# A batched 64x64 matmul: both loads as fp32 from SyncE, casts moved to the engines, a two-stage pipeline

## The chip, the cores and the metric

One core of one Trainium2 chip. The metric is device time in microseconds (us) of that core. Most executions of a kernel agree within a fraction of a per cent; a run more than 1.5% above the fastest of its kernel is marked slow and is not used in a comparison. Rates are decimal GB/s; sizes of loads in KB and MB are powers of two, as the traces count them.

Some terms. HBM is the memory of the chip; SBUF is the core's own, in 128 partitions; PSUM is where TensorE (PE in the profile) leaves its results. A DMA is one copy between HBM and SBUF. An engine (GpSimd, SyncE or ScalarE) issues it, and the core's 16 DMA engines carry it out in packets. A load "lands" as its bytes reach SBUF. VectorE is DVE in the profile, ScalarE is ACT, GpSimd is POOL.

## The reference

```python
def setup_inputs():
    return {"a": np.random.randn(1024, 64, 64).astype(np.float32),
            "b": np.random.randn(1024, 64, 64).astype(np.float32)}

def reference(a, b):
    return np.matmul(a, b).astype(np.float32)
```

a, b and the output are 16.78 MB each, so 50.3 MB pass between HBM and the core, at very little arithmetic.

## The kernel before

The 1024 products are done in 16 tiles of 64. A tile of a is 1 MB, loaded in four DMAs (`h`) of 256 KB by GpSimd, which casts fp32 to bf16 on the way; a tile of b is one DMA of 1 MB by SyncE, still fp32, cast later by VectorE. Both sit in a pool of four tiles.

```python
    a_v = a.rearrange("(t g h) (mp v) k -> t h g mp (v k)", h=4, g=16, v=8)
    b_v = b.rearrange("(t g h) (kp u) n -> t (h kp) g (u n)", h=4, g=16, u=2)
    ...
    def load(t):
        a_sb = a_pool.tile([128, 4, 8, 64], bf16, name="a_sb")
        for h in range(4):
            nc.gpsimd.dma_start(
                out=a_sb[:, h, :, :].rearrange("p v k -> p (v k)"), in_=a_v[t, h]
            )
        b_sb = b_pool.tile([128, 16, 128], fp32, name="b_sb")
        nc.sync.dma_start(out=b_sb[:], in_=b_v[t])
    ...
    for t in range(n_t):
        load(t + AHEAD)                                   # if there is such a tile
        nc.vector.tensor_copy(a_bf[:], ...a_sb...)        # bf16 reorder
        # 16 transposes of a on PE, PSUM copied out half by VectorE, half by ScalarE
        for h in range(4):                                # block-diagonal weights
            nc.vector.tensor_copy(at_bd[rows, :, h, :], at_v[rows, :, :])
        nc.vector.tensor_copy(b_bf[:], b_sb[:])           # fp32 -> bf16
        for gq in range(4):
            ...                                           # 16 matmuls
            nc.scalar.copy(o_sb[:, gq, :, :, :], o_ps[:])
        nc.gpsimd.dma_start(out=o_v[t], in_=...o_sb...)   # 1 MB
```

(Cut and abridged: the comments with "..." stand for code that the argument does not touch.)

Of the kernel before, what the change touches and what calls it, by code (L numbers as in the profile page):

```python
# [1 line left out]

# [5 lines left out]

fp32 = mybir.dt.float32
bf16 = mybir.dt.bfloat16  # L10


@with_exitstack
def kernel(
    ctx: ExitStack,
    tc: tile.TileContext,
    a: bass.AP,
    b: bass.AP,
    out: bass.AP,
):  # L20





    nc = tc.nc
    B, M, K = a.shape
    _, _, N = b.shape
    assert (M, K, N) == (64, 64, 64) and B % 64 == 0

    T = 64
    n_t = B // T
    AHEAD = 3

    a_v = a.rearrange("(t g h) (mp v) k -> t h g mp (v k)", h=4, g=16, v=8)
    b_v = b.rearrange("(t g h) (kp u) n -> t (h kp) g (u n)", h=4, g=16, u=2)
    o_v = out.rearrange("(t g h) (mo w) n -> t (h mo) g (w n)", h=4, g=16, w=2)

    consts = ctx.enter_context(tc.tile_pool(name="consts", bufs=1))
    a_pool = ctx.enter_context(tc.tile_pool(name="a_pool", bufs=AHEAD + 1))  # L40
    b_pool = ctx.enter_context(tc.tile_pool(name="b_pool", bufs=AHEAD + 1))
    work = ctx.enter_context(tc.tile_pool(name="work", bufs=2))
    o_pool = ctx.enter_context(tc.tile_pool(name="o_pool", bufs=3))
    t_psum = ctx.enter_context(
        tc.tile_pool(name="t_psum", bufs=4, space=bass.MemoryType.PSUM)
    )
    o_psum = ctx.enter_context(
        tc.tile_pool(name="o_psum", bufs=4, space=bass.MemoryType.PSUM)
    )

    bd_tiles = [
        consts.tile([128, 64, 4, 32], bf16, name=f"at_bd{i}") for i in range(2)
    ]
    a_tiles, b_tiles = {}, {}

    def load(t):
        a_sb = a_pool.tile([128, 4, 8, 64], bf16, name="a_sb")
        for h in range(4):
            nc.gpsimd.dma_start(  # L59
                out=a_sb[:, h, :, :].rearrange("p v k -> p (v k)"), in_=a_v[t, h]  # L60
            )
        b_sb = b_pool.tile([128, 16, 128], fp32, name="b_sb")
        nc.sync.dma_start(out=b_sb[:], in_=b_v[t])
        a_tiles[t], b_tiles[t] = a_sb, b_sb

    load(0)
    identity = consts.tile([128, 128], bf16)
    make_identity(nc, identity)
    for bd in bd_tiles:
        nc.vector.memset(bd[:], 0.0)  # L70
    for t in range(1, AHEAD):
        load(t)

    for t in range(n_t):
        if t + AHEAD < n_t:
            load(t + AHEAD)
        a_sb, b_sb, at_bd = a_tiles.pop(t), b_tiles.pop(t), bd_tiles[t % 2]

        a_bf = work.tile([128, 8, 4, 64], bf16, name="a_bf")
        nc.vector.tensor_copy(a_bf[:], a_sb[:].rearrange("p h v k -> p v h k"))  # L80
        a_cols = a_bf[:].rearrange("p v h k -> p v (h k)")

        at_sb = work.tile([128, 2, 2, 128, 4], bf16, name="at_sb")
        for w in range(2):
            at_ps = t_psum.tile([128, 4, 2, 128], bf16, name="at_ps")
            for vo in range(4):
                for u in range(2):
                    nc.tensor.transpose(  # L88
                        at_ps[:, vo, u, :], a_cols[:, 2 * vo + w, u::2], identity[:]
                    )  # L90
            for u in range(2):
                dst = at_sb[:, w, u, :, :]
                src = at_ps[:, :, u, :].rearrange("p vo q -> p q vo")
                if u == 0:
                    nc.vector.tensor_copy(dst, src)  # L95
                else:
                    nc.scalar.copy(dst, src)  # L97
        at_v = at_sb[:].rearrange("p w u (g mp) vo -> p (w u g) (mp vo)", g=16)
        for h in range(4):
            rows = slice(32 * h, 32 * h + 32)  # L100
            nc.vector.tensor_copy(at_bd[rows, :, h, :], at_v[rows, :, :])  # L101
        b_bf = work.tile([128, 16, 128], bf16, name="b_bf")
        nc.vector.tensor_copy(b_bf[:], b_sb[:])  # L103
        o_sb = o_pool.tile([128, 4, 4, 2, 64], fp32, name="o_sb")
        for gq in range(4):
            o_ps = o_psum.tile([128, 4, 2, 64], fp32, name="o_ps")
            for g4 in range(4):
                g = 4 * gq + g4
                for w in range(2):
                    for u in range(2):  # L110
                        nc.tensor.matmul(  # L111
                            o_ps[:, g4, w, :],
                            at_bd[:, (2 * w + u) * 16 + g, :, :].rearrange(
                                "p h mo -> p (h mo)"
                            ),
                            b_bf[:, g, 64 * u : 64 * u + 64],
                            start=(u == 0),
                            stop=(u == 1),
                        )
            nc.scalar.copy(o_sb[:, gq, :, :, :], o_ps[:])  # L120

        nc.gpsimd.dma_start(  # L122
            out=o_v[t], in_=o_sb[:].rearrange("p q g w n -> p (q g w n)")
        )


# [1 line left out]
_INS = ['a', 'b']  # L128
_OUTS = [((1024, 64, 64), 'float32')]


# [23 lines left out]
```

## Time and profile before

| | before |
|---|---|
| time, median of 3 runs | 151.15 us |
| span of the profiled run | 148.9 us |
| busiest engines | VectorE 70% of the span, PE 43%, GpSimd 42%, ScalarE 36% |
| last load lands / last store lands | 121.6 / 147.1 us |

Parts of the profile page of the kernel before: busy times (us, share of the span, instructions), the busy tenths of the DMA engines in 40 slices, the GB/s of those slices, and the DMA queues (packets, MB, share of 16 engines' span).

```profile
PE 64.4 (43%) x1280; PEld 62.0 (42%) x1280; DVE 104.9 (70%) x130; ACT 53.5 (36%) x97; POOL 62.6 (42%) x86
...
DMA  3999999999999999999999999999999995892594
GB/s 77 292 290 292 291 293 293 295 286 276 293 364 383 322 291 275 370 308 290 283 348 366 309 292 287 368 310 291 294 321 369 195 356 207 237 273 68 169 265 129
...
q0 software_dynamic: 13568, 25.17, 66.7%
q1 hardware_dynamic: 8448, 16.78, 33.2%
```

The DMA row is full until about 123 us, and no engine is. So DMA bounds this kernel, then a tail does. The GB/s row needs care: it counts bytes **as they land**. Queue 0 carries 25.17 MB although it reads a (16.78 MB) and writes the output (16.78 MB): a counts at 8.39 MB, because it lands as bf16. So a slice with 292 GB/s and no stores reads more than 292 from HBM: counted in the trace's packet records from 8 to 32 us, 91 GB/s of a and 200 of b land, so 383 are read.

Two stretches of the same trace: without stores, and the tail. The columns are start:end, length, busy time of each engine, granted clock of PE, busy share of the DMA engines (over 1 when packets overlap), GB/s.

```profile
8.00:32.00 24.00, 11.84 (x192) 11.31 (x192) 16.95 (x22) 6.94 (x12) 10.09 (x17) 1.00 1.13 292
121.00:148.00 27.00, 13.91 (x285) 13.62 (x282) 13.78 (x20) 11.28 (x20) 4.92 (x4) 0.69 0.70 211
```

Two of the groups of instructions that the change touches (engine, operation, out<-in, shapes and types, count, then busy us, mean ns, then the engine's idle time just before them and what ended it):

```profile
L103 DVE CAST b_bf<-b_sb 128x2048 bf16<-128x2048 f32 x16 | 19.3, 1226 | 2.2 <-PE o_ps L111 2.2
L80 DVE COPY a_bf<-a_sb 128x2048 bf16<-128x2048 bf16 x16 | 10.8, 694 | 8.7 <-DMA a_sb<-in_a_dram 7.7
```

### The profile page before, as it was taken

The page shows a single profiled execution, that of the slowest core. Times are in us where ns is not written, and L with a number is a line of the kernel's source. Part 1 is how long each engine was busy: PE and PEld are TensorE (multiplying, and loading weights), DVE is VectorE, ACT ScalarE, POOL GpSimd, SP SyncE. Part 2 cuts the span into 40 slices and gives each one's busy share as a digit, 9 for nine tenths or more (in the row PEclk, how much of TensorE's full clock was granted, in tenths as well). Part 3 has the DMA queues.
Part 4 walks back from the last instruction along what each step waited for, and adds up shares of the span by engine and source line. Part 5 has one row for each costly group of instructions (what it writes and reads, how often), then busy time and mean ns, then how long its engine had stood idle before and what let it go on. Part 6 is the DMA issues. An engine that isn't in the chain of part 4 may idle for free.

```text
span 148.9 us, 3081 instructions
## 1 busy us (share of the span) xinstructions
PE 64.4 (43%) x1280; PEld 62.0 (42%) x1280; DVE 104.9 (70%) x130; ACT 53.5 (36%) x97; POOL 62.6 (42%) x86
## 2 busy tenths in 40 slices
PE   0005225960893058500990079402990059429400
PEld 0004215950893058500890078302880059429400
DVE  5754499799978297938995498919985497994000
ACT  3000052763320914064502733082602827616500
POOL 7644364336622165712983174614754303300410
PEclk9999999998569758955598557965599556975865
DMA  3999999999999999999999999999999995892594
GB/s 77 292 290 292 291 293 293 295 286 276 293 364 383 322 291 275 370 308 290 283 348 366 309 292 287 368 310 291 294 321 369 195 356 207 237 273 68 169 265 129
DMA packets 22031, 42.15 MB, mean 283 GB/s; under 512 B 1537, under 2 KB 9729, under 8 KB 22017
## 3 DMA queue, kind: packets, MB, share of 16 engines
q0 software_dynamic: 13568, 25.17, 66.7%
q1 hardware_dynamic: 8448, 16.78, 33.2%
q8 instruction: 10, 0.16, 0.4%
q14 instruction: 5, 0.03, 0.1%
HBM read 33.55 MB, written 16.78 MB: 338 GB/s over the span
## 4 chain that ended last, share of the span: by engine, by line
DMA 52%; issue 19%; POOL 11%; DVE 5%; PE 4%; ACT 3%; POOLq 1%; ACTq 0%; DVEq 0%
DMA a_sb<-in_a_dram 44%; POOL out_dram L122 8%; DMA out_dram<-o_sb 8%; PE o_ps L111 4%; POOL a_sb L59 2%; DVE at_sb L95 2%; DVE at_bd L101 2%; ACT at_sb L97 2%; ACT o_sb L120 1%; POOLq L150 1%; DVE b_bf L103 1%; DVE a_bf L80 0%; POOL identity masks.py:199 0%; POOL identity masks.py:197 0%; POOLq L122 0%
## 5 line engine op out<-in xcount | busy, mean ns | idle before, releaser
L111 PE MATMUL o_ps<-b_bf,at_bd 128*128 128x64 bf16 x1024 | 48.1, 225 | 59.3 <-DVE at_bd L101 59.3
L111 PEld LDWEIGHTS <-at_bd 128*128 128x128 bf16 x1024 | 46.6, 120 | 61.3 <-DVE at_bd L101 61.3
L59 POOL DMA_DIRECT2D a_sb<-in_a_dram x64 | 41.4, 652 | 50.8 <-DMA a_sb<-in_a_dram 23.7
L101 DVE COPY at_bd<-at_sb 32x2048 bf16<-32x2048 bf16 x64 | 49.7, 776 | 17.5 <-ACT at_sb L97 16.6
L120 ACT COPY o_sb<-o_ps 128x512 f32<-128x512 f32 x64 | 35.6, 591 | 65.7 <-PE o_ps L111 33.5
L122 POOL DMA_DIRECT2D out_dram<-o_sb x16 | 20.6, 1290 | 28.2 <-ACT o_sb L120 21.9
L97 ACT COPY at_sb<-at_ps 128x512 bf16<-128x512 bf16 x32 | 17.4, 624 | 20.2 <-DVE at_sb L95 20.0
L88 PE MATMUL at_ps<-identity,a_bf 128*128 128x128 bf16 x256 | 17.4, 231 | 15.8 <-DVE a_bf L80 15.8
L88 PEld LDWEIGHTS <-a_bf 128*128 128x128 bf16 x256 | 15.9, 104 | 16.1 <-DVE a_bf L80 16.1
L103 DVE CAST b_bf<-b_sb 128x2048 bf16<-128x2048 f32 x16 | 19.3, 1226 | 2.2 <-PE o_ps L111 2.2
L95 DVE COPY at_sb<-at_ps 128x512 bf16<-128x512 bf16 x32 | 19.9, 680 | 0.0
L80 DVE COPY a_bf<-a_sb 128x2048 bf16<-128x2048 bf16 x16 | 10.8, 694 | 8.7 <-DMA a_sb<-in_a_dram 7.7
L70 DVE MEMSET at_bd<- 128x4096 uint32 x2 | 6.9, 3472 | 2.5 <-PEq L139 1.7
L97 ACT ACT_TABLE_LOAD x1 | 1.3, 1283 | 0.7 <-PEq L139 0.7
masks.py:199 POOL TENSOR_SCALAR_AFFINE_SELECT identity<-identity 128x128 bf16<-128x128 bf16 x1 | 0.4, 364 | 0.0
masks.py:197 POOL MEMSET identity<- 128x128 bf16 x1 | 0.3, 266 | 0.0
L139 POOL MEMSET const-float32-0.0<- 128x1 f32 x1 | 0.1, 98 | 0.2 <-issue 0.2
L139 POOL MEMSET const-bfloat16-1.0<- 128x1 bf16 x1 | 0.1, 101 | 0.0
L139 POOL MEMSET const-uint8-127<- 128x1 uint8 x1 | 0.1, 101 | 0.0
L139 POOL MEMSET const-float32-1.0<- 128x1 f32 x1 | 0.1, 98 | 0.0
## 6 DMA issues: line engine op xcount, KB each, us to landing
out_dram<-o_sb POOLq DMA_DIRECT2D x16, 1024.0 KB, 10.9
a_sb<-in_a_dram POOLq DMA_DIRECT2D x64, 128.0 KB, 11.7
b_sb<-in_b_dram SPq DMA_DIRECT2D x16, 0.5 KB, 14.8
```

Source lines behind the costliest of these rows:

```text
L59: nc.gpsimd.dma_start(out=a_sb[:, h, :, :].rearrange("p v k -> p (v k)"), in_=a_v[t, h])
L70: nc.vector.memset(bd[:], 0.0)
L80: nc.vector.tensor_copy(a_bf[:], a_sb[:].rearrange("p h v k -> p v h k"))
L88: nc.tensor.transpose(at_ps[:, vo, u, :], a_cols[:, 2 * vo + w, u::2], identity[:])
L95: nc.vector.tensor_copy(dst, src)
L97: nc.scalar.copy(dst, src)
L101: nc.vector.tensor_copy(at_bd[rows, :, h, :], at_v[rows, :, :])
L103: nc.vector.tensor_copy(b_bf[:], b_sb[:])
L111: nc.tensor.matmul(o_ps[:, g4, w, :], at_bd[:, (2 * w + u) * 16 + g, :, :].rearrange("p h mo -> p (h mo)"), b_bf[:, g, 64 * u : 64 * u + 6 ...
L120: nc.scalar.copy(o_sb[:, gq, :, :, :], o_ps[:])
L122: nc.gpsimd.dma_start(out=o_v[t], in_=o_sb[:].rearrange("p q g w n -> p (q g w n)"))
L150: with _tile.TileContext(nc) as tc:
```

## The change

The intent: take the loads off GpSimd, so that it only issues stores; let SyncE issue both loads as plain fp32; split the casts between VectorE (a) and ScalarE (b); prepare tile t+1 before multiplying tile t; and store the last tile in four parts.

```diff
-        a_sb = a_pool.tile([128, 4, 8, 64], bf16, name="a_sb")
+        a_sb = a_pool.tile([128, 4, 8, 64], fp32, name="a_sb")
         for h in range(4):
-            nc.gpsimd.dma_start(
+            nc.sync.dma_start(
                 out=a_sb[:, h, :, :].rearrange("p v k -> p (v k)"), in_=a_v[t, h]
             )
 ...
+        b_bf = work.tile([128, 16, 128], bf16, name="b_bf")
+        nc.scalar.copy(b_bf[:], b_sb[:])
 ...
-        b_bf = work.tile([128, 16, 128], bf16, name="b_bf")
-        nc.vector.tensor_copy(b_bf[:], b_sb[:])
 ...
+            if last:
+                nc.gpsimd.dma_start(
+                    out=o_v[t, :, 4 * gq : 4 * gq + 4, :], ...
 ...
+    prepare(0)
+    for t in range(n_t):
+        if t + AHEAD < n_t:
+            load(t + AHEAD)
+        if t + 1 < n_t:
+            prepare(t + 1)
+        multiply(t)
```

(Also: three block-diagonal buffers instead of two, `AHEAD` 4 instead of 3 with the same four buffers for each of a and b, and every second copy of the last output on VectorE.)

## The prediction

> **What bounds the kernel now.** The DMA engines, then an unfilled tail. The page's DMA row is 9 in nearly every slice to about 123 us and falls apart after; DVE is 70% busy, PE 43%, ACT 36%, POOL 42%. HBM traffic is 50.3 MB (33.55 read, 16.78 written). Counting DMA packet records per 4 us window and solving for the engine time of each kind gives about 0.082 us for a 2 KB "a" read cast by the DMA, 0.089 us for a 2 KB "b" packet of 512 B rows, 0.17 us for a 4 KB store packet. Over 16 engines: 42 + 46 + 43.5 = 131 us, near 385 GB/s. The span is 148.9 us, so DMA idles some 16 us: 2.4 at the head, the rest in the tail. Timeline: the last load lands near 121.7 us, when only about 11.3 of 16.78 MB are stored. The scheduler works on tiles in pairs, so the last tiles go through DVE, PE, ACT and store pair after pair; the last stores are issued at 137.5 and 140.7 us and land by 147 us.
>
> **What the change removes, adds, moves.**
> - 64 "a" issues leave GpSimd (41.4 us busy, off the bound) for SyncE. The Trainium skill, "DMA: Bandwidth & Descriptors", section "Issuing engines are not separate DMA queues", says that this adds no bandwidth; the trace agrees so far: all queue mixes give 375 to 390 GB/s. "a" now lands as fp32: HBM bytes are unchanged, SBUF-side bytes rise by 8.4 MB. I expect 0.080 us per "a" packet, transfer still near 130 us. I trust this term least.
> - DVE: "a" cast from fp32, about 1.23 us (as b's today) instead of 0.69; b's cast leaves (-1.23); one more 3.5 us memset at the start. About 5.5 us a tile, 100 us in all: below DMA.
> - ACT: b's cast, 1.85 us estimated from 0.49 us per 512 columns back to back; about 5.4 us a tile, 85 us in all.
> - Three block-diagonal buffers and "prepare(t+1) before multiply(t)": in the instruction order the first nine tiles go in threes, the last six or so one by one. So 12 to 13 MB are stored when the last load lands, and the tail is one tile deep.
> - Last store in four parts: the last quarter needs about 2.5 us after its copy, instead of 6.4.
>
> **Critical path after.** First bytes at 2.4 us; loads with about 12.5 MB of stores at 380 to 387 GB/s end at 123 to 126 us (later than now, since more stores precede them); then the last tile: b cast 1.9, evacuation 1.2, four block copies 2.8, matmuls 3.3, copy 0.6, issue and landing 3.5: 13 to 15 us, DMA partly busy with stores. Last landing near 139.5, span near 141, reported time about 2 us more.
>
> **Prediction: 143.5 us, 8 in 10 between 138 and 148.** Chances: faster by over 2% 0.86; within 2% 0.12; slower by over 2% 0.02.
>
> **What would show it.** Right: DMA row full to about 124 us; last load near 124 us, last store within 16 us of it; DVE about 70%, ACT about 60%, POOL far below 42%; b packets still about 0.09 us; the chain mostly DMA with a short DVE/PE/ACT end. Wrong: HBM rate in full windows outside 375 to 395 GB/s; DMA gaps mid-run, from casts that in-order DVE or ACT takes ahead of older tiles' work.
>
> **What would make it wrong.** Faster: plain 2 KB packets from one hardware queue run near 410 GB/s (about 137 us). Slower: fp32 landing in SBUF, or one queue for both loads, lowers the rate to 370 GB/s; or loads stall because SyncE issues in order, each behind the eighth before it and a buffer's cast.

## More of the kernel before

The source of one a DMA, `a_v[t, h]`, is **16 blocks** of 16 KB, 64 KB apart in HBM; each block gives eight partitions a row of 2 KB each. The source of one b DMA is 128 partitions times 16 **pieces of 512 B**.

VectorE hardly waits for data: 7.7 us for a in the whole run.

## The result, and the profile after

The changed kernel takes **173.94 us** (median of 4 runs, 173.18 to 174.69), the kernel before 151.1 us beside it. The ratio is 1.149 (95% interval 1.139 to 1.159). Here and below, a ratio is the mean time of one kernel's fast runs over that of the other's in the same rounds, so not quite the ratio of the medians. The prediction, 143.5 us and 138 to 148, was wrong by 30 us and in direction.

The same parts of the page, after:

```profile
PE 75.8 (44%) x1280; PEld 70.5 (41%) x1280; DVE 100.5 (58%) x117; ACT 79.3 (46%) x111; POOL 23.3 (14%) x25
...
DMA  4999999999999999999999999999999999994294
GB/s 127 258 259 273 258 266 263 271 315 328 369 305 280 374 275 339 373 338 256 375 278 288 348 310 346 285 370 366 337 361 290 301 337 275 376 311 165 74 273 144
...
q1 hardware_dynamic: 17664, 33.56, 69.5%
q0 software_dynamic: 4400, 16.78, 27.7%
```

The DMA row is as full as before, yet the kernel is slower. Nothing is cast in flight now, so landed and HBM bytes are the same: where no stores run, the loads move 256 to 273 GB/s, and where stores run beside them, the sum still reaches 375. The two stretches:

```profile
8.00:32.00 24.00, 8.04 (x93) 7.25 (x94) 14.82 (x15) 6.45 (x8) 0.00 (x0) 1.00 1.03 264
155.00:171.00 16.00, 6.59 (x113) 6.31 (x110) 6.21 (x8) 5.50 (x8) 4.17 (x5) 0.61 0.59 175
```

264 GB/s of HBM instead of 383, with the DMA engines busy all the time and PE at full clock. The tail went as planned: from the last load to the last store it is 15.3 us long, not 25.5. The two casts:

```profile
L70 DVE CAST a_bf<-a_sb 128x2048 bf16<-128x2048 f32 x16 | 21.1, 1321 | 50.0 <-DMA a_sb<-in_a_dram 49.9
L89 ACT CAST b_bf<-b_sb 128x2048 bf16<-128x2048 f32 x16 | 30.5, 1904 | 41.0 <-DMA b_sb<-in_b_dram 41.0
```

The casts cost what was foreseen (1.32 and 1.90 us; foreseen 1.23 and 1.85). But VectorE now waits 49.9 us for a, ScalarE 41.0 us for b. The last load lands at 155.3 us (before: 121.6), the last store at 170.6. So 33.7 us are lost before the last load lands, and about 10 won after it.

### The profile page after: what moved, and what is told of

Same layout as the page of the kernel before. It is cut to its first block, busy times and chain, and to the rows that moved or that the text cites. A ratio compares the mean times of both kernels' runs of the same rounds, so it can differ in the third digit from the quotient of the medians.

```text
span 172.1 us, 3073 instructions
## 1 busy us (share of the span) xinstructions
PE 75.8 (44%) x1280; PEld 70.5 (41%) x1280; DVE 100.5 (58%) x117; ACT 79.3 (46%) x111; POOL 23.3 (14%) x25
## 3 DMA queue, kind: packets, MB, share of 16 engines
q1 hardware_dynamic: 17664, 33.56, 69.5%
## 4 chain that ended last, share of the span: by engine, by line
issue 39%; SPq 18%; DMA 15%; DVE 12%; POOL 8%; PE 4%; ACT 1%; POOLq 1%; DVEq 0%
SPq L60 16%; DMA a_sb<-in_a_dram 15%; DVE at_bd L94 8%; POOL out_dram L125 7%; PE o_ps L106 4%; DVE a_bf L70 3%; DVE at_sb L85 1%; POOL out_dram L120 1%; SPq L64 1%; ACT o_sb L118 1%; ACT at_sb L87 1%; POOLq L168 0%; DVEq L70 0%; POOLq L125 0%; POOLq L120 0%
## 5 line engine op out<-in xcount | busy, mean ns | idle before, releaser
L106 PE MATMUL o_ps<-b_bf,at_bd 128*128 128x64 bf16 x1024 | 49.8, 226 | 27.7 <-DVE at_bd L94 27.7
L106 PEld LDWEIGHTS <-at_bd 128*128 128x128 bf16 x1024 | 47.6, 121 | 30.5 <-DVE at_bd L94 30.3
L78 PE MATMUL at_ps<-identity,a_bf 128*128 128x128 bf16 x256 | 27.1, 290 | 62.4 <-DVE a_bf L70 62.4
L94 DVE COPY at_bd<-at_sb 32x2048 bf16<-32x2048 bf16 x64 | 47.9, 749 | 6.9 <-ACT at_sb L87 6.1
L70 DVE CAST a_bf<-a_sb 128x2048 bf16<-128x2048 f32 x16 | 21.1, 1321 | 50.0 <-DMA a_sb<-in_a_dram 49.9
L78 PEld LDWEIGHTS <-a_bf 128*128 128x128 bf16 x256 | 23.3, 135 | 64.8 <-DVE a_bf L70 64.8
L89 ACT CAST b_bf<-b_sb 128x2048 bf16<-128x2048 f32 x16 | 30.5, 1904 | 41.0 <-DMA b_sb<-in_b_dram 41.0
L125 POOL DMA_DIRECT2D out_dram<-o_sb x15 | 19.6, 1307 | 140.9 <-ACT o_sb L118 140.9
L133 DVE MEMSET at_bd<- 128x4096 uint32 x3 | 10.4, 3472 | 3.3 <-PEq L157 1.7
L120 POOL DMA_DIRECT2D out_dram<-o_sb x4 | 3.0, 756 | 3.1 <-ACT o_sb L118 2.6
L116 DVE COPY o_sb<-o_ps 128x512 f32<-128x512 f32 x2 | 1.4, 692 | 3.0 <-PE o_ps L106 3.0
```

The costliest lines, as they stand in the source:

```text
L70: nc.vector.tensor_copy(a_bf[:], a_sb[:].rearrange("p h v k -> p v h k"))
L78: nc.tensor.transpose(at_ps[:, vo, u, :], a_cols[:, 2 * vo + w, u::2], identity[:])
L89: nc.scalar.copy(b_bf[:], b_sb[:])
L106: nc.tensor.matmul(o_ps[:, g4, w, :], at_bd[:, (2 * w + u) * 16 + g, :, :].rearrange("p h mo -> p (h mo)"), b_bf[:, g, 64 * u : 64 * u + 6 ...
L120: nc.gpsimd.dma_start(out=o_v[t, :, 4 * gq : 4 * gq + 4, :], in_=o_sb[:, gq, :, :, :].rearrange("p g w n -> p (g w n)"),)
L125: nc.gpsimd.dma_start(out=o_v[t], in_=o_sb[:].rearrange("p q g w n -> p (q g w n)"))
```

## The experiments

Theories in the texts. **Q**: one hardware queue for both loads is the limit. **W**: what is limited is the rate at which bytes land in SBUF, about 290 GB/s whatever the shape. **C**: the interplay with the computing. Later, when W fell: **L**, the length of a partition's run; **H**, the 64 KB steps in HBM; **P**, the number of blocks in the source (the idea being that it decides how rows are dealt to the 16 DMA engines); **S**, pieces of 512 B; **G**, gaps or short blocks in HBM.

Four kernels only load: phases with a barrier after each, each tile touched once by VectorE so that its landing is waited for, then stores of zeros. Their outputs are wrong, which doesn't matter for the times. Only the rates inside the phases count. They ran once each (state unknown); their clock stayed at 1.00.

### Which half of the change: the pipeline alone, and the loads alone

Pipeline alone, the changed kernel with a loaded as before:

```diff
-        a_sb = a_pool.tile([128, 4, 8, 64], fp32, name="a_sb")
+        a_sb = a_pool.tile([128, 4, 8, 64], bf16, name="a_sb")
-            nc.sync.dma_start(out=a_sb[:, h, ...], in_=a_v[t, h])
+            nc.gpsimd.dma_start(out=a_sb[:, h, ...], in_=a_v[t, h])
```

> The changed kernel with a loaded as before (GpSimd, cast to bf16 in the DMA); pipeline, b cast on ScalarE and split last store stay. If the new loads are the cause (Q and W alike): 140 to 147 us, as the prediction had it. If the new order of work is the cause: above 165 us.

Measured: 143.29 us, ratio to the kernel before 0.949 (0.942 to 0.956), correct. This is the time that the prediction gave for the whole change. In its trace, the stretch without stores and the tail:

```profile
8.00:32.00 24.00, 10.35 (x153) 9.44 (x154) 17.09 (x21) 10.22 (x13) 10.75 (x18) 1.00 1.13 293
121.00:140.00 19.00, 6.72 (x198) 6.19 (x194) 9.55 (x15) 9.06 (x15) 5.70 (x6) 0.87 0.84 258
```

293 landed again, as before the change, and the last load lands at 121.4 us; the gain is in the tail.

Loads alone, the kernel before with the a tile as fp32 and `nc.sync` in place of `nc.gpsimd` (VectorE then casts both):

> The kernel before with only the loads changed: a as fp32 from SyncE, cast on VectorE. If the loads are the cause: 168 to 180 us, with 260 to 275 GB/s in stretches without stores. If the new order is the cause: near 151 us.

Measured: 177.34 us, ratio 1.163 (1.153 to 1.173; two of its four runs were slow and are left out of the ratio). The stretch without stores (the profiled run was one of the slow ones):

```profile
8.00:32.00 24.00, 9.82 (x176) 9.12 (x176) 15.45 (x18) 6.60 (x12) 1.89 (x2) 1.00 1.06 266
```

The loads lost everything, and the new order of work was innocent. With the slow loads the new order also gains little: 1.163 without it and 1.149 with it, intervals that overlap, where with the old loads it gained 5%.

### The queue: a as fp32 from GpSimd

The changed kernel with `nc.gpsimd.dma_start` for a, the tile still fp32.

> The changed kernel with a still landing as fp32 but issued from GpSimd, so two queues. Theory Q: the rate is back near 385 GB/s and the time near 140 to 148 us. Theory W: stays near 165 to 175 us, near 265 to 290 GB/s without stores.

Measured: 171.27 us, ratio 1.130 (1.124 to 1.137). The stretch without stores, loads now from two queues:

```profile
8.00:32.00 24.00, 7.35 (x80) 6.57 (x81) 14.14 (x14) 5.76 (x7) 9.12 (x15) 1.00 1.05 257
```

Theory Q falls. With the same issuer as before the change and only the cast removed from the DMA, the rate is 257 GB/s.

### Loads by themselves

```diff
+    phase(nc.sync,   None,    a_t)  # 1: a alone, fp32
+    phase(None,      nc.sync, a_t)  # 2: b alone
+    phase(nc.sync,   nc.sync, a_t)  # 3: both on SyncE
+    phase(nc.scalar, nc.sync, a_t)  # 4: a on ScalarE's queue
+    phase(nc.gpsimd, nc.sync, a_t)  # 5: a fp32 from GpSimd
+    phase(nc.gpsimd, nc.sync, c_t)  # 6: a cast to bf16 by GpSimd's DMA
```

> Wrong result on purpose: no matmul, only loads in six phases with a barrier after each (6 tiles; each of a and b is 1 MB a tile), then stores of zeros. 1: a alone on SyncE; 2: b alone on SyncE; 3: both on SyncE, as the changed kernel; 4: a on ScalarE's queue, b on SyncE; 5: a fp32 from GpSimd, b on SyncE; 6: a cast to bf16 by GpSimd's DMA, b on SyncE, as the kernel before. Rates read from HBM. Theory Q (one hardware queue is the limit): phases 1 to 3 near 265 GB/s, phases 4 to 6 near 385. Theory W (bytes landing in SBUF are the limit, about 290 GB/s): phases 3, 4 and 5 all near 265 to 290, only phase 6 near 385 (290 landed). Theory C (it is neither, but the interplay with the computing): phase 3 near 385.

The six phases in this order (columns here: length, busy time of VectorE and GpSimd, clock, DMA share, GB/s landed):

```profile
14.00:28.00 14.00, 2.15 (x14) 0.00 (x0) 1.00 1.06 268
40.00:52.00 12.00, 0.46 (x3) 0.00 (x0) 1.00 1.05 289
66.00:100.00 34.00, 3.08 (x20) 0.00 (x0) 1.00 1.06 257
120.00:148.00 28.00, 2.61 (x18) 0.00 (x0) 1.00 1.06 288
166.00:194.00 28.00, 2.16 (x16) 7.29 (x14) 1.00 1.05 261
214.00:238.00 24.00, 2.95 (x21) 7.70 (x15) 1.00 1.13 292
```

No computing is needed for the slow rate: theory C falls. Each load is slow alone, 268 and 289. Two hardware queues help a little (288 against 257), GpSimd's queue does not (261). Only with the cast in flight does HBM deliver 384 GB/s (92 of a and 200 of b land), and there too 292 GB/s land. Everything so far fits theory W.

### Does anything land faster?

The same 6 MB of a from SyncE, plain fp32, each partition one contiguous run of 2, 4, 8, 16 KB and the runs adjacent in HBM; then the kernel's own a pattern, cast by GpSimd, alone.

```diff
+    rows(nc.sync, 2)   # src = flat.rearrange("(d p r) -> d p r", p=128, r=512)
+    rows(nc.sync, 4)
+    rows(nc.sync, 8)
+    rows(nc.sync, 16)
+    cast()
```

> Wrong result on purpose: loads only, 6 MB of a in each of five phases, then stores of zeros. 1 to 4: plain fp32 from SyncE, each partition one contiguous run of 2, 4, 8, 16 KB, and the runs of neighbouring partitions adjacent in HBM; 5: the kernel's own a pattern (2 KB rows), cast to bf16 by GpSimd's DMA, alone. Theory W (bytes landing in SBUF, any shape): phases 1 to 4 all at 265 to 292 GB/s, phase 5 at 340 to 400 read (half landed). Theory L (length of the run decides): phase 1 near 270, rising to 390 or more by 8 to 16 KB. Theory H (the kernel's HBM order, blocks of 16 KB at 64 KB steps, is what is slow): phase 1 already near 385.

```profile
13.00:21.00 8.00, 1.85 (x12) 0.00 (x0) 1.00 1.05 391
30.00:38.00 8.00, 0.93 (x6) 0.00 (x0) 1.00 1.03 417
48.00:58.00 10.00, 0.61 (x4) 0.00 (x0) 1.00 1.01 427
68.00:76.00 8.00, 0.31 (x2) 0.00 (x0) 1.00 1.01 432
90.00:95.00 5.00, 1.08 (x8) 3.59 (x7) 1.00 1.24 201
```

Theory W falls in its general form: 391 to 432 GB/s of fp32 land. The very row length of the kernel, 2 KB, lands at 391 when the source is one run. L explains the rise from 391 to 432, not the fall to 268. The last line is 201 landed, so 402 read: the kernel's a pattern is no burden to HBM.

### Steps in HBM, or the shape of the transfer?

```diff
+    a_phase(a as the kernel: 16 blocks of 16 KB, steps of 64 KB)   # 1
+    a_phase(the same, steps of 66 KB)                              # 2
+    a_phase(the same, steps of 20 KB)                              # 3
+    b_phase(b as the kernel: 512 B pieces, steps of 64 KB)         # 4
+    b_phase(the same, steps of 66 KB)                              # 5
+    b_phase(512 B pieces out of one contiguous 1 MB)               # 6
```

(In words; SyncE, fp32. In phases 4 to 6 the pieces have small gaps between them in SBUF, so that they stay pieces; phase 4 is then the control.)

> Wrong result on purpose: plain fp32 loads from SyncE in six phases with a barrier after each. 1: a as the kernel loads it (16 blocks of 16 KB at 64 KB steps, 2 KB a partition); 2: the same with the blocks at 66 KB steps; 3: the same at 20 KB steps; 4: b as the kernel loads it (512 B pieces, 16 to a partition at 64 KB steps); 5: the same at 66 KB steps; 6: 512 B pieces from one contiguous 1 MB. Theory W (any fp32 landing is held to 290) has fallen with the row phases (2 KB rows from contiguous HBM landed at 391). Theory H (the 64 KB step in HBM): phase 1 near 268, phases 2 and 3 near 390; phase 4 near 290, phase 5 and 6 well above. Theory P (which engine writes which partitions, the same in phases 1 to 3 since each source has 16 blocks): phases 1, 2, 3 all near 268. Theory S (512 B pieces are slow to land): phases 4, 5, 6 all near 290.

```profile
10.00:27.00 17.00, 2.61 (x17) 0.00 (x0) 1.00 1.06 288
36.00:48.00 12.00, 1.84 (x12) 0.00 (x0) 1.00 1.05 283
60.00:74.00 14.00, 2.22 (x15) 0.00 (x0) 1.00 1.06 289
82.00:98.00 16.00, 0.61 (x4) 0.00 (x0) 1.00 1.05 297
108.00:120.00 12.00, 0.46 (x3) 0.00 (x0) 1.00 1.04 295
128.00:144.00 16.00, 0.62 (x4) 0.00 (x0) 1.00 1.02 297
```

Theory H falls: the step does not matter for either load. P and S stand. Phase 1 is the load that gave 268 in the first phase of "Loads by themselves", and here it gives 288. These were single executions on different chips, and the difference is not explained, so differences of less than a tenth between such runs are not read.

### 128 rows cut into 128, 64, 32 or 16 blocks

One pattern, 128 rows of 2 KB out of the same 320 KB, differing only in how many equal blocks the rows form.

```diff
+    a_phase(nc.sync,   x, 128)  # 1: blocks in the source
+    a_phase(nc.sync,   x, 64)   # 2
+    a_phase(nc.sync,   x, 32)   # 3
+    a_phase(nc.sync,   x, 16)   # 4: as the kernel's a
+    a_phase(nc.gpsimd, x, 128)  # 5
+    a_phase(nc.gpsimd, x, 16)   # 6
+    a_phase(nc.gpsimd, c, 16)   # 7: cast to bf16
+    b_phase(y1, 8)              # 8: contiguous HBM, pieces of 1 KB
+    b_phase(y2, 4)              # 9: pieces of 2 KB
```

> Wrong result on purpose: loads only. Phases 1 to 4 (fp32, SyncE): 128 rows of 2 KB to 128 partitions out of the same 320 KB of HBM, cut in 128, 64, 32 and 16 blocks with gaps between blocks. 5 and 6: 128 and 16 blocks, fp32, from GpSimd; 7: 16 blocks, cast to bf16, GpSimd. 8 and 9: contiguous HBM landing in pieces of 1 KB and 2 KB. Theory P (the number of blocks in the source decides how rows and partitions are dealt to the 16 DMA engines, and dealing by 16 makes fp32 land slowly): phase 1 near 390, phase 4 near 287, 2 and 3 at one or the other; the same from GpSimd (5 fast, 6 slow); 7 near 400, since half the bytes land. Rival G (gaps or short blocks in HBM are slow by themselves): phases 1 and 4 about equal, near 287. Pieces: 8 between 300 and 390, 9 near 390.

```profile
12.00:20.00 8.00, 1.84 (x12) 0.00 (x0) 1.00 1.05 394
36.00:42.00 6.00, 1.36 (x9) 0.00 (x0) 1.00 1.05 393
56.00:62.00 6.00, 1.38 (x9) 0.00 (x0) 1.00 1.05 393
75.00:88.00 13.00, 2.15 (x14) 0.00 (x0) 1.00 1.06 286
102.00:110.00 8.00, 1.72 (x12) 5.36 (x10) 1.00 1.03 391
120.00:136.00 16.00, 2.46 (x16) 7.26 (x14) 1.00 1.03 273
150.00:156.00 6.00, 1.38 (x9) 4.08 (x8) 1.00 1.24 201
165.00:173.00 8.00, 0.46 (x3) 0.00 (x0) 1.00 1.09 353
180.00:185.00 5.00, 0.31 (x2) 0.00 (x0) 1.00 1.05 396
```

A clean step: 394, 393, 393, then 286 at 16 blocks from SyncE, and the same step from GpSimd (391 against 273). G falls, since gaps do no harm at 128, 64 or 32 blocks. With the cast the same 16 blocks read at 402. And pieces: 297 at 512 B (the run before), 353 at 1 KB, 396 at 2 KB.

Why 16 blocks land slowly is not shown. The Trainium skill, "DMA: Bandwidth & Descriptors", section "Why a DMA increments its semaphore by 16 and not by 1", says that the number of DMA engines of a transfer follows from the slowest dimension of both access patterns; by that, 16, 32 and 128 blocks all use 16 engines. Which rows then go to which engine it gives, under "The descriptor swizzle", for a 128-partition transfer, where each engine writes partitions of one SBUF port. A deal in runs of eight partitions would not have that property. That is a guess: no record of these traces tells which engine wrote which partition.

### Is it so in the kernel? The changed kernel with other source orders

First a alone, then b too. The bytes, tiles and engine work are those of the changed kernel; the values land in the wrong places. Their outputs are wrong, which doesn't matter for the times.

```diff
-    a_v = a.rearrange("(t g h) (mp v) k -> t h g mp (v k)", h=4, g=16, v=8)
+    a_v = a.rearrange("(t h g) (mp v) k -> t h (g mp) (v k)", h=4, g=16, v=8)   # 128 rows, one run
 # second run only:
-    b_v = b.rearrange("(t g h) (kp u) n -> t (h kp) g (u n)", h=4, g=16, u=2)
+    b_v = b.rearrange("(t c) (kp u) n -> t (c kp) (u n)", c=64, u=32)            # 8 KB a partition
```

> Wrong result on purpose: the changed kernel, with only the HBM order of a altered, so that each a load is 128 rows of 2 KB from one 256 KB run[...] instead of 16 blocks. Same bytes, same work on every engine. Theory P: load-only stretches near 336 GB/s (a at 391, b still at about 295), load packets near 0.098 us instead of 0.125; from engine time about 100 us of loads and 44 of stores, plus head and tail: 153 to 163 us. If the a pattern is not the matter in the kernel: 171 to 176 us.

> Wrong result on purpose: as the run before it, and b also altered, to one 8 KB run a partition instead of 16 pieces of 512 B. Theory P with S (512 B pieces): both loads fast although all of it lands as fp32; load-only stretches near 400 GB/s, 137 to 145 us. If fp32 landing is slow by itself beside the kernel's computing (theory W again): above 165 us.

Measured: 156.04 us (ratio to the kernel before 1.030, 1.025 to 1.034) with a altered, 142.41 us (0.936, 0.930 to 0.943) with both. Both inside what was expected. The same stretch, first of one, then of the other (its profiled run was a slow one, 1.5% above its fastest). Their first stores start at 30.6 and 30.2 us, just inside it; from 8 to 30 us the rates are 326 and 405:

```profile
8.00:32.00 24.00, 11.60 (x176) 10.80 (x176) 20.86 (x23) 12.48 (x17) 1.71 (x1) 0.96 1.05 327
```

```profile
8.00:32.00 24.00, 12.05 (x202) 11.12 (x202) 22.03 (x24) 13.47 (x18) 1.94 (x2) 1.00 1.03 404
```

So 264, 327, 404 GB/s, and 174, 156, 142 us, with all of it landing as fp32 from one hardware queue and being cast by the engines. Neither fp32 by itself nor SyncE nor the casts are at fault. The two shapes are, when they land as plain fp32: about 18 us by a's blocks and 14 us by b's pieces.

### Three that were meant to improve, or to price a part

**a in one run, done correctly.** The batch dealt as `(t h g)` makes each a load one run of HBM, with right results; but then b and the stores must be cut into four DMAs of 32 partitions.

```diff
+    a_v = a.rearrange("(t h g) (mp v) k -> t h (g mp) (v k)", ...)
-        nc.sync.dma_start(out=b_sb[:], in_=b_v[t])
+        for h in range(4):
+            nc.sync.dma_start(out=b_sb[32 * h : 32 * h + 32], in_=b_v[t, h])
+        # stores likewise, four of 32 partitions
```

> The changed kernel with the batch dealt so that each a load is 256 KB in one run of HBM, 128 rows of 2 KB (a source of 128 rows, not of 16 blocks); this forces b and the stores to be cut into four DMAs of 32 partitions each, which can cost something of its own. Theory P: load-only stretches above 300 GB/s (391 for a, at most 295 for b, about 336 mixed) and a time of 150 to 165 us, unless 32-partition DMAs are slow. If the a pattern is not the matter: 172 us or more.

Measured: 192.77 us, ratio 1.275 (1.268 to 1.281), correct: a miss, and slower than all others. b now shows up in packets of 512 B of mean 0.043 us where it had packets of 2 KB; four of them make 0.17 us. It says nothing about a: the remedy costs more than the ill.

**Both loads cast in the DMA by GpSimd**, b's cast on ScalarE gone.

```diff
-        b_sb = b_pool.tile([128, 16, 128], fp32, name="b_sb")
-        nc.sync.dma_start(out=b_sb[:], in_=b_v[t])
+        b_sb = b_pool.tile([128, 16, 128], bf16, name="b_sb")
+        nc.gpsimd.dma_start(out=b_sb[:], in_=b_v[t])
```

(Also: six buffers for b instead of four.)

> The changed kernel with both a and b cast to bf16 by DMAs from GpSimd; no b cast on ScalarE. Landed bytes fall to 16.8 MB. Theory W: no landing limit left, HBM rate 375 to 400 GB/s, 138 to 146 us (engine packet times bound it as in the pipeline-only run at 143.3). If GpSimd's issuing of 80 loads and 19 stores bounds instead: above 150 us with GpSimd busy or waiting throughout.

Measured: 151.46 us, ratio 1.001 (0.997 to 1.005), correct: a miss. From 8 to 24 us 188 GB/s land, so 376 are read, as expected; its last load (b) lands at 127.7 us, 6.3 us later than with the pipeline alone, and its last store only at 148.1 us, 8.6 later. So the rate came out as theory W had it and the time did not. That GpSimd's issuing bounds is not shown either: it was busy for 54% of the span, and of its waits 20.8 us were for the outputs of ScalarE. Why its last tiles come at intervals of 8 to 10 us was not followed up.

**The pipeline with the last store whole**, `last = False` (which also leaves all copies of the last output to ScalarE).

> The pipeline-only run with the last store whole instead of in 4 parts. If the split was worth what the prediction said (about 4 us off the end: 2.5 us instead of 6.4 us after the last copy): 146 to 148 us. If the pipeline alone carries the gain: within 1 us of 143.3.

Measured: 143.01 us over six runs, ratio 0.948 (0.944 to 0.951): the four-part store is worth nothing. The last store lands at 139.4 us whole and at 139.5 us in parts. Tile 14's store is issued only at 129.6 us, so, as we read the trace, at the end the DMA engines have 2 MB to write either way, at the 258 GB/s of the tail line above, and the four parts are issued one after the other by GpSimd, 0.75 us each.

## Why the prediction was wrong, point by point

- **What bounds the kernel before** was read rightly: DMA to 122 us, then a tail with DMA partly idle.
- **The step that failed** is the term of a's transfer: "I expect 0.080 us per "a" packet, transfer still near 130 us. I trust this term least." In the stretch without stores the changed kernel moves 264 GB/s, so a 2 KB load packet takes on average 16 x 2048 B / 264 GB/s = 0.124 us. The page after gives the load queue 69.5% of 172.1 us, so about 120 us of all 16 engines, where packets of 0.080 and 0.089 us foresaw 41 + 46 = 87: these 33 us are about the size of the miss. "b packets still about 0.09 us" failed with it: b alone moves 289 GB/s, 0.113 us a packet, and 295 to 297 in other orders of HBM.
- **How it came to fail.** The packet times, 0.082 and 0.089 us, were solved from stretches in which a landed at half its bytes. They were taken for properties of reading a and b, and only the read side stays the same in this change. What the runs showed is that each of these two shapes alone lands at 268 to 297 GB/s as fp32, a because its source has 16 blocks, b because of its 512 B pieces; with a cast in flight, 91 + 200, about 292, land while 383 are read. The mix was even kind to b: by the packet records its 2 KB packets took 0.095 us beside the cast a (before, 8 to 32 us) and 0.119 us alone. The page gave a hint: 290 to 295 in the slices without stores. That landing also limited the kernel before is the natural reading of the equal numbers, 292 with the cast and 289 for b alone, but it is argued, not shown.
- **Of the ways to be wrong that it named**, "fp32 landing in SBUF, or one queue for both loads, lowers the rate to 370 GB/s" came nearest: the first half was right in kind, the size was 264, and the condition was missing, since fp32 lands at 391 from one run. The second half was wrong (257 with two queues, and 404 from one). The third way, loads that stall because SyncE issues in order, is not the cause: SyncE did wait about 29 us for VectorE before loads of a, but the DMA row stayed full, with no computing the same loads move 257 GB/s, and with the other source orders the same order of issue moves 404.
- **That more issuers add no bandwidth** is from the Trainium skill, "DMA: Bandwidth & Descriptors", section "Issuing engines are not separate DMA queues". This agrees for GpSimd beside SyncE (257 and 261 against 264 and 257); ScalarE beside SyncE gave 288 against 257, so a tenth more, in one run. "All queue mixes give 375 to 390 GB/s" was a little narrow: in windows of 4 us, while its DMA row is full, the kernel before moves 346 to 396 GB/s of HBM.
- **VectorE and ScalarE** were right: 100.5 and 79.3 us busy, foreseen 100 and 85. Neither came to bound.
- **The pipeline and the tail** were right: alone it gives 143.29 us, forecast 143.5, and in the changed kernel the last store lands 15.3 us after the last load (forecast 13 to 16). But in the pipeline alone the loads did not end later for the stores' sake (121.4 us with 12.0 MB stored by then; forecast 123 to 126 with 12.5), and the tail was 18.1 us instead of 13 to 15. That its total is so close is in part luck: the two misses cancel.
- **The four-part store** was overrated: 6.4 us down to 2.5 was forecast, 0 measured. That the stores' transfer and not the last one's latency ends the run is a reading of the trace, not tested.
- The sum, as an estimate: the last load went from 121.6 to 155.3 us, of which about 7 us are the 2.8 MB of stores that now come before it (14.1 instead of 11.3 MB, at 385 GB/s) and the rest slow landing; the tail gave about 10 us back.

The version that beats both is the pipeline with a still cast by GpSimd's DMA: 143.0 to 143.3 us.

## What to carry to other kernels

When a DMA that casts is replaced by a plain one, its landed bytes double though HBM's do not: look up the landed rate before, and ask whether the destination can take more. Two transfers of the same bytes, partitions and row length can differ by more than a quarter with the shape of the source (394 against 286 GB/s): measure a new load shape alone, in a kernel that only loads, before the kernel is built on it. A packet time solved from a mix of streams holds for that mix only.

## What the Trainium skill lacked or had wrong

- "DMA: Bandwidth & Descriptors", "Why a DMA increments its semaphore by 16 and not by 1": the slowest dimensions are said to set the number of engines. That the shape can set the speed where this rule gives the same number is missing: 128 rows of 2 KB to 128 partitions as plain fp32 land at 393 to 394 GB/s from 128, 64 or 32 source blocks, at 286 from 16.
- The same page, "Specifications", gives 512 B and more as the size for line rate. In these loads pieces of 512 B landed at 297 GB/s, 1 KB at 353, 2 KB at 396, one run of 16 KB a partition at 432.
- The same page, "SWDGE vs HWDGE vs iDMA", ties casts to GpSimd but does not say what a cast in flight is worth: with 16 source blocks it read 402 GB/s where the plain load got 268 to 288.
- "SBUF — State Buffer", the box on the "DVE blocks DMA" trap in "SBUF: two separate sides", advises to move loads from GpSimd to SyncE or ScalarE to keep VectorE from starving them. It does not say that the move gives up a cast in the DMA. Here that was the cost, and not the move: the changed kernel takes 143.29 us with a cast by GpSimd's DMA, 171.27 us with a as fp32 from GpSimd and 173.94 us as fp32 from SyncE. The casting loads kept the DMA row full beside a VectorE that was 70% busy; whether VectorE's work was of the kind that the box means, no run shows.
